# Two gain vectors moved from the activations: the input norm's g into the split of the transposed tiles, the heads' g into the split of the output weights

## The chip, the cores and the metric

The kernel runs on one core of a Trainium2 chip. The metric is the device time of one execution in microseconds (us), the median of several runs. Everything is float32; matrix products are made from a high and a low part of each operand, three TensorE passes per product (high × high, high × low, low × high), so each operand has to be split into two tiles, `h` and `l`.

## The reference

One layer of a streaming encoder, applied to 1024 prompt tokens and to 32 sample tokens with a state. Cut to what matters here:

```python
def rms_norm(x, g):
    y = x * rsqrt(mean(x * x, -1) + EPS)
    return y * g                              # g: one factor per feature (1024)

xn   = rms_norm(x, g_mix_pre)
proj = xn @ w_in                              # (tokens, 1024) @ (1024, about 3700)
...                                           # three groups of heads: GLA, HGRN2, mLSTM
o_a  = head_rms_norm(o_a, g_a) * silu(gr)     # per head: normed, times g_head, times a gate
o_b  = head_rms_norm(o_b, g_b) * silu(hg)
o_c  = head_rms_norm(h,   g_c) * sigmoid(mo)
x    = x + rms_norm(concat(o_a, o_b, o_c) @ w_out, g_mix_post)
x    = x + rms_norm(conv_ffn(rms_norm(x, g_ffn_pre)), g_ffn_post)
```

`g_mix_pre` scales the features over which the first product sums, and `g_head` the features over which the product with `w_out` sums. Each can therefore be applied to either operand of its product.

## The kernel before, in words

Tokens are handled in units of 128 (unit 8 holds the 32 sample tokens), and units in three groups: units 0 to 2, units 3 to 5, units 6, 7 and 8.

For each group the in-projection runs in stages. `scale_x` loads x of a unit (tokens on the partitions, 1024 features along), sums its squares on ScalarE (ACT), forms 1/rms on GpSimd (POOL: `rstd_of`, L221 and L222) and scales x on VectorE (DVE) by that column and by `gx`, a copy of g_mix_pre on every partition (L310 for unit 0, in two halves; L319 for the others). `norm_group` transposes the unit on TensorE, 128 features at a time and four such tiles to a PSUM bank, and splits each bank into `xh` (ACT, L333) and `xl` (DVE, L334), 512 columns in one instruction each. Then come the products: `vg` makes eight blocks of 256 columns with tokens on the partitions (`vg_across` for the third group), `feat` makes tiles of 128 features. Blocks 4 to 7 are the gates. `vg_store` turns a gate's PSUM tile into `vth` (or `gth` in the third group) with tanh on ACT (L113, called at L437) and one or two DVE instructions (L440, L442), multiplies it on POOL by `gh`, half of g_head copied to every partition (L444, out to the tile `vg`), and stores it to `g_d` in DRAM with POOL's queue (L445). `vth` has one buffer, `gth` three, `vg` three. Values (blocks 0 to 3) are copied to `vg` by ACT and stored to `v_d`.

`scale_x` of the next group runs behind block 5 of a group: its Square and scaling are ordered behind the last tanh and the last DVE instruction of `vg_store` (`vgi`). The mixers of a group run interleaved with the in-projection of the next one; they read `g_d` back as `gt` and multiply the normed heads by it (L1019).

`gx` is loaded by ACT's DMA queue first of all (512 KB written), `gh` by SP's queue behind the constants (L652, 512 KB) and halved on DVE (L653). `out_weights` splits the eight tiles of w_out, 128 rows of 1024 each, into `woh` (ACT, L107 or L1075) and `wol` (DVE, L110 or L1077), one tile for each k of the first unit's product in the out-projection (`outproj`). `split` is the helper of L107 and L110; `mm3` that of L101 to L103.

The order of the instructions on each engine is worked out by a planner from a simulated timeline; `high_priority` and `issue_after` in the code bend it.

Of the kernel before, what the change touches and what calls it, by code (L numbers as in the profile page):

```python
# [8 lines left out]
F32 = mybir.dt.float32  # L9
# [3 lines left out]
AF = mybir.ActivationFunctionType  # L13
ALU = mybir.AluOpType
# [40 lines left out]
for _h in (0, 2, 1, 3, 4):  # L55
# [24 lines left out]

TC = dict(schedule_with_timeline_sim=True)
IN_NAMES = ["xp", "xs", "w_feat", "w_tok0", "w_tok", "w_out", "w_up", "w_dn", "vecs", "gcols", "grows", "wg",
            "mconv", "mcache", "fconv", "fcache", "s_gh", "s_c", "s_m", "rowb", "masks", "cf"]
# [8 lines left out]
def body(ctx: ExitStack, tc: tile.TileContext, a: dict):  # L92
# [12 lines left out]
    def split(hi, lo, src, eng=None, heng=None):  # L105
        if heng is None:
            act.copy(hi, src)  # L107
        else:
            heng.tensor_copy(hi, src)
        (eng or pool).tensor_tensor(lo, src, hi.bitcast(F32), op=ALU.subtract)  # L110
# [50 lines left out]
            sp.dma_start(t, src)  # L161
        return t

    gx = p1.tile([128, 1024], F32, name="gx")
    act.dma_start(gx, a["grows"][3:4, :].broadcast_to([128, 1024]))
# [86 lines left out]
    gh = p1.tile([128, 1024], F32, name="gh")  # L252

    cols_of, dcs_of, behind = {}, {}, {}
    HSET = (2, 0, 4, 5)
# [37 lines left out]
    def scale_x(g):  # L293
        for (u, off, n) in units_of(g):
            x = x_in.pop(u, None)
            x = load_x(u) if x is None else x
            if g == 0:
                jk = mx.tile([128, 1024], BF16, tag=("gt", "cat", "k")[u], name=f"jk{u}", bufs=1)
            else:
                jk = mx.tile([128, 1024], BF16, tag="qe", name=f"jk{u}", bufs=1)  # L300
            rs = p1.tile([128, 1], F32, tag="rs", name=f"rs{u}", bufs=2)
            if u == 0:
                ss = p1.tile([128, 2], F32, name="ss0")
                hs = slice(0, 512), slice(512, 1024)
                for i, c in enumerate(hs):
                    act.activation(jk[:, c], x[:, c], AF.Square, scale=1.0 / 32, accum_out=ss[:, i:i + 1])
                pool.tensor_scalar(rs, ss[:, 0:1], ss[:, 1:2], EPS, op0=ALU.add, op1=ALU.add)
                pool.tensor_tensor(rs, rs, mhalf[:, :1], op=ALU.pow)
                for c in hs:
                    dve.scalar_tensor_tensor(x[:, c], x[:, c], rs, gx[:, c], op0=ALU.mult, op1=ALU.mult)  # L310
                xn_of[u] = x
                yield
                continue
            ss = p1.tile([128, 1], F32, tag="ss", name=f"ss{u}", bufs=2)
            with tc.issue_after(vgi[0].ins) if vgi else ExitStack():
                act.activation(jk[:n], x[:n], AF.Square, accum_out=ss[:n])
            rstd_of(rs[:n], ss[:n], n, 1, 1024)
            with tc.issue_after(vgi[1].ins) if vgi else ExitStack():
                dve.scalar_tensor_tensor(x[:n], x[:n], rs[:n], gx[:n], op0=ALU.mult, op1=ALU.mult)  # L319
            xn_of[u] = x  # L320
            yield

    def norm_group(g, xh, xl):
        for (u, off, n) in units_of(g):
            x = xn_of[u]
            for hf in range(2):
                ps = psb.tile([128, 4, 128], F32, tag="big", name=f"xt{u}{hf}")
                for k in range(4):
                    c = 512 * hf + 128 * k
                    pe.transpose(ps[:, k, :n], x[:n, c:c + 128], ident[:n, :n])  # L330
                s = slice(4 * hf, 4 * hf + 4), slice(off, off + n)
                with tc.high_priority(offset=AHEAD):
                    act.copy(xh[(slice(None), *s)], ps[:, :, :n])  # L333
                    dve.tensor_tensor(xl[(slice(None), *s)], ps[:, :, :n], xh[(slice(None), *s)].bitcast(F32), op=ALU.subtract)  # L334
# [34 lines left out]
    def inproj(g, xh, xl, normed, scaled=None):  # L369
# [55 lines left out]
            return ws  # L425

        def vg_store(blk, u, off, n, ps):
            o = mx.tile([128, 256], F32, tag="vg", name=f"vg{u}_{blk}", bufs=3)
            t = t0 + off
            if blk < 4:  # L430
                vcopies.append(act.copy(o[:n], ps[:n, :256]))
                (act if g or blk else pool).dma_start(v_d[t:t + n, 256 * blk:256 * blk + 256], o[:n])
                return
            c0 = 256 * (blk - 4)
            th = gate[0].tile([128, 256], F32, tag="gth", name=f"gth{u}_{blk}", bufs=3) if gate else \
                mx.tile([128, 256], F32, tag="vth", name=f"vth{u}_{blk}", bufs=1)
            ia = tanh(th[:n], ps[:n, :256], 0.5)  # L437
            ns = min(max(704 - c0, 0), 256)
            if ns:
                iv = dve.scalar_tensor_tensor(th[:n, :ns], th[:n, :ns], 1.0, ps[:n, :ns], op0=ALU.add, op1=ALU.mult)  # L440
# [3 lines left out]
            pool.tensor_tensor(o[:n], th[:n], gh[:n, c0:c0 + 256], op=ALU.mult)  # L444
# [202 lines left out]
        dve.scalar_tensor_tensor(er[R], fm[R], -1.0, fm[R], op0=ALU.mult, op1=ALU.min)  # L647
        act.activation(er[R], er[R], AF.Exp)
        yield

        if g == 0:
            sp.dma_start(gh, a["grows"][2:3, :].broadcast_to([128, 1024]))  # L652
            dve.tensor_scalar(gh, gh, 0.5, None, op0=ALU.mult)  # L653


        for t, f in ((6, 1), (7, 2)):
            ps = feat(t)
# [409 lines left out]

    def out_weights(W):
        for k in range(8):
            if k < 2:  # L1070
                split(W[1][k], W[2][k], wo_raw[k], dve)
            else:

                with tc.issue_after(halves[0].ins):
                    act.copy(W[1][k], wo_raw[k])  # L1075
                with tc.issue_after(halves[1].ins):
                    dve.tensor_tensor(W[2][k], wo_raw[k], W[1][k].bitcast(F32), op=ALU.subtract)  # L1077
            yield


# [787 lines left out]
def _layout(i):  # L1868
# [28 lines left out]
    grows = np.stack([np.asarray(i["g_mix_post"])[0], np.asarray(i["g_ffn_post"])[0], np.asarray(i["g_head"])[0],  # L1897
                      np.asarray(i["g_mix_pre"])[0]])
    wg = np.zeros((128, 192), f)
    wg[64:80] = np.asarray(i["gla_w_gate"])[0]  # L1900

# [45 lines left out]
    r = dict(xp=np.asarray(i["x_prompt"])[0], xs=np.asarray(i["x_sample"])[0], w_feat=w_feat, w_tok0=w_tok0, w_tok=w_tok, w_out=w_out,  # L1947
             w_up=w_up, w_dn=w_dn, vecs=vecs, gcols=gcols, grows=grows, wg=wg, mconv=mconv, mcache=mcache, fconv=fconv,
             fcache=fcache, s_gh=s_gh, s_c=s_c, s_m=s_m, rowb=rowb, masks=masks, cf=cf)
    return {k: np.ascontiguousarray(v) for k, v in r.items()}  # L1950
# [43 lines left out]
```

## Time and profile before

| | |
|---|---|
| median of 3 runs | 1357.33 us (1355.49 to 1357.98) |
| profiled execution, first to last instruction | 1355.3 us |
| TensorE busy | 1310.8 us, 97% |
| VectorE (DVE) busy | 1025.2 us, 76% |
| ScalarE (ACT) busy | 709.8 us, 52% |
| GpSimd (POOL) busy | 317.6 us, 23% |
| mean granted TensorE clock | 0.983 of full speed |
| DMA | 269.72 MB, mean 199 GB/s |

The profiled execution's own time is known as its span only; the median of the timed runs lies 2.0 us above that. In rows of the timeline the columns are start, duration, engine, line, operation, output and inputs, how many were merged, and in brackets how long the engine had been idle before and what released it. In rows of a line's instructions the three durations are the shortest, the median and the longest in ns, then the first and the last start in us and the shapes. PE is TensorE's matmuls, PEld its weight loads.

### The profile page before, as it was taken

How to read it: one execution, taken by the hardware profiler on the slowest of the kernel's cores; microseconds unless marked ns; L12 is line 12 of the kernel's file. 1: busy time of each engine (PE TensorE's matmuls, PEld its weight loads, DVE VectorE, ACT ScalarE, POOL GpSimd, SP SyncE). 2: the span in 40 equal slices, each digit the busy share in tenths (PEclk: the TensorE clock that was granted, in tenths of full speed). 3: DMA queues.
4: the chain of work that ended last, by engine and by line, in shares of the span. 5: the costliest groups of instructions: out<-in, count | busy, mean ns of one | idle time of the engine just before them, and what ended most of it. 6: DMA issues, size and time to landing. Idle time of an engine off the chain costs nothing.

```text
span 1355.3 us, 29229 instructions
## 1 busy us (share of the span) xinstructions
PE 1310.8 (97%) x11472; PEld 1196.7 (88%) x11472; DVE 1025.2 (76%) x1921; ACT 709.8 (52%) x1362; POOL 317.6 (23%) x530
## 2 busy tenths in 40 slices
PE   6999999999999999999999999999999999999997
PEld 5999889998888887767899999999999996678885
DVE  5795649768598678876998888888888876499566
ACT  5555556555574555435654554545554545454552
POOL 4532303135032254213211212111111110010005
PEclk9999999999998989989999999999999999999998
DMA  9799778886879963454315457536455239645435
GB/s 342 241 358 363 265 244 258 278 281 211 292 230 308 336 201 125 142 182 103 128 48 188 134 133 189 134 111 180 120 147 154 82 127 397 254 161 146 141 102 124
DMA packets 126881, 269.72 MB, mean 199 GB/s; under 512 B 24167, under 2 KB 59143, under 8 KB 126663
## 3 DMA queue, kind: packets, MB, share of 16 engines
q1 hardware_dynamic: 113111, 244.78, 53.2%
q0 software_dynamic: 9120, 18.62, 7.3%
q10 hardware_dynamic: 4512, 4.46, 1.0%
q8 instruction: 90, 1.47, 0.5%
q14 instruction: 48, 0.39, 0.1%
HBM read 206.72 MB, written 86.18 MB: 216 GB/s over the span
## 4 chain that ended last, share of the span: by engine, by line
PE 63%; DVE 5%; DMA 3%; ACT 3%; issue 2%; POOL 1%; SPq 0%; DVEq 0%; POOLq 0%; ACTq 0%
PE pux L103 5%; PE pux L102 5%; PE pux L101 5%; PE puw L101 3%; PE puw L103 3%; PE puw L102 3%; PE q L101 3%; PE q L102 3%; PE q L103 3%; PE x L101 2%; PE x L102 2%; PE x L103 2%; PE puz L103 2%; PE puz L101 2%; PE puz L102 2%
## 5 line engine op out<-in xcount | busy, mean ns | idle before, releaser
L1409 DVE SCALAR_TENSOR_TENSOR y<-uu,fconv_sb,y 128x1060 f32<-128x1060 f32 x88 | 116.2, 1320 | 36.8 <-ACT y L1407 36.2
L1345 ACT COPY c<-pux 128x272 f32<-128x272 f32 (+1 forms) x132 | 49.3, 375 | 50.5 <-PE pux L103 49.8
L1407 ACT ACTIVATE y<-uu,fconv_sb 128x1060 f32<-128x1060 f32 x44 | 56.1, 1275 | 8.5 <-POOL uu L1403 7.8
L101 PE MATMUL pv<-wt_0h,xh 128*128 128x256 f32 (+1 forms) x192 | 56.3, 293 | 3.6 <-DVE xl L334 1.6
L103 PE MATMUL zp<-woh,cl 128*128 128x512 f32 (+1 forms) x144 | 57.7, 401 | 1.5 <-DVE cl L1106 1.5
L1406 POOL COPY fhalo<-uu 128x2 f32<-128x2 f32 x44 | 16.6, 376 | 180.7 <-DVE uu L1350 180.6
L101 PE MATMUL zp<-woh,ch 128*128 128x512 f32 (+1 forms) x144 | 57.8, 410 | 0.8 <-ACT ch L1105 0.8
L102 PE MATMUL zp<-wol,ch 128*128 128x512 f32 (+1 forms) x144 | 57.9, 402 | 0.0
L103 PE MATMUL pv<-wt_1h,xl 128*128 128x256 f32 (+1 forms) x192 | 55.1, 287 | 0.0
L103 PE MATMUL pv<-wt_0h,xl 128*128 128x256 f32 (+1 forms) x192 | 55.0, 286 | 0.0
L102 PE MATMUL pv<-wt_0l,xh 128*128 128x256 f32 (+1 forms) x192 | 54.8, 286 | 0.0
L101 PE MATMUL pv<-wt_1h,xh 128*128 128x256 f32 (+1 forms) x192 | 54.7, 285 | 0.0
L102 PE MATMUL pv<-wt_1l,xh 128*128 128x256 f32 (+1 forms) x192 | 54.4, 283 | 0.0
L1585 POOL TENSOR_TENSOR gss<-gss 128x1 f32<-128x1 f32 (+1 forms) x9 | 8.2, 906 | 185.0 <-ACT gjk L1578 185.0
L221 POOL TENSOR_SCALAR hrs<-hss 128x5 f32<-128x5 f32 (+3 forms) x27 | 10.1, 375 | 176.5 <-DVE hss L1015 172.6
L831 DVE COPY_PREDICATED P<-masks_sb,sc 128x352 f32<-128x352 int32 (+3 forms) x53 | 37.9, 715 | 5.9 <-PE sc L744 5.0
L101 PEld LDWEIGHTS pv<-wt_0h,xh 128*128 128x128 f32 x192 | 36.4, 190 | 5.3 <-DVE xl L334 2.1
L1403 POOL COPY uu<-uu 128x2 f32<-128x2 f32 x44 | 28.0, 637 | 38.8 <-DVE uu L1350 37.8
L101 PEld LDWEIGHTS pv<-wt_1h,xh 128*128 128x128 f32 x192 | 36.2, 189 | 0.7 <-issue 0.6
L222 POOL TENSOR_TENSOR hrs<-hrs,mhalf 128x5 f32<-128x5 f32 (+3 forms) x27 | 36.2, 1341 | 2.2
L103 PEld LDWEIGHTS pv<-wt_0h,xl 128*128 128x128 f32 x192 | 36.5, 190 | 0.2
L102 PEld LDWEIGHTS pv<-wt_0l,xh 128*128 128x128 f32 x192 | 36.5, 190 | 0.1
(1743 smaller groups left out, 5321.0 us busy)
## 6 DMA issues: line engine op xcount, KB each, us to landing
wrP<-in_w_dn SPq DMA_DIRECT2D x27, 512.0 KB, 4.4
h_d<-y SPq DMA_DIRECT2D x22, 530.0 KB, 3.7
ht<-h_d SPq DMA_DIRECT2D x22, 530.0 KB, 10.5
wt_0r<-in_w_tok SPq DMA_DIRECT2D x21, 512.0 KB, 5.7
wt_1r<-in_w_tok SPq DMA_DIRECT2D x21, 512.0 KB, 6.3
ws_d<-in_w_dn POOLq DMA_DIRECT2D x20, 512.0 KB, 8.9
wrP<-ws_d SPq DMA_DIRECT2D x20, 512.0 KB, 4.0
wt_0l<-lt_d SPq DMA_DIRECT2D x14, 512.0 KB, 4.5
```

The costliest lines, as they stand in the source:

```text
L101: pe.matmul(ps, lh[0], rh[0], start=first, stop=False, **kw)
L102: pe.matmul(ps, lh[0], rh[1], start=False, stop=False, **kw)
L103: return pe.matmul(ps, lh[1], rh[0], start=False, stop=last, **kw)
L221: pool.tensor_scalar(out, ss, 1.0 / width, eps, op0=ALU.mult, op1=ALU.add)
L222: pool.tensor_tensor(out, out, mhalf[:n, :cols], op=ALU.pow)
L831: dve.copy_predicated(dst, mk.broadcast_to([n, 11, *mk.shape[2:]]), src)
L1345: kept[name] = act.copy(t, ps)
L1403: pool.tensor_copy(u[:, GAP_P:GAP_P + 2], u[:, GAP_S - 2:GAP_S])
L1406: behind["POOL"] = pool.tensor_copy(fhalo[:, j, :], u[:, NCOL - 2:NCOL])
L1407: act.activation(y, u, AF.Identity, scale=fconv[:, j, 2:3], bias=fconv[:, j, 3:4])
L1409: dve.scalar_tensor_tensor(y, uu[i][:, s:s + NCOL], fconv[:, j, s:s + 1], y, op0=ALU.mult, op1=ALU.add)
L1585: pool.tensor_tensor(ss[:n, 0:1], ss[:n, 2:3], ss[:n, 3:4], op=ALU.add)
```

## The change

Both gains become columns: `gin` is [128, 2, 8], one column for each tile of 128 features, for g_mix_pre (`gmix`) and g_head (`ghead`, halved once on DVE). x is scaled by 1/rms alone. After the transposes features lie on the partitions, so g_mix_pre is applied as a per-partition factor while the tile is split; the split of a bank becomes four pairs of instructions of 128 columns. g_head is applied in the split of w_out's rows. The gates are stored as DVE leaves them, from one tile (`vg` with four buffers, or `gth` with three), which values use too.

```diff
-    gx = p1.tile([128, 1024], F32, name="gx")
-    act.dma_start(gx, a["grows"][3:4, :].broadcast_to([128, 1024]))
+    gin = cp.tile([128, 2, 8], F32, name="gin_sb")
+    act.dma_start(gin, a["gin"])
+    gmix, ghead = gin[:, 0], gin[:, 1]
...
+    dve.tensor_scalar(ghead, ghead, 0.5, None, op0=ALU.mult)
...
                 for c in hs:
-                    dve.scalar_tensor_tensor(x[:, c], x[:, c], rs, gx[:, c], op0=ALU.mult, op1=ALU.mult)
+                    dve.tensor_scalar(x[:, c], x[:, c], rs, None, op0=ALU.mult)
...
-                dve.scalar_tensor_tensor(x[:n], x[:n], rs[:n], gx[:n], op0=ALU.mult, op1=ALU.mult)
+                dve.tensor_scalar(x[:n], x[:n], rs[:n], None, op0=ALU.mult)
...
-                s = slice(4 * hf, 4 * hf + 4), slice(off, off + n)
                 with tc.high_priority(offset=AHEAD):
-                    act.copy(xh[(slice(None), *s)], ps[:, :, :n])
-                    dve.tensor_tensor(xl[(slice(None), *s)], ps[:, :, :n], xh[(slice(None), *s)].bitcast(F32), op=ALU.subtract)
+                    for k in range(4):
+                        c, gk = (slice(None), 4 * hf + k, slice(off, off + n)), gmix[:, 4 * hf + k:4 * hf + k + 1]
+                        act.activation(xh[c], ps[:, k, :n], AF.Copy, scale=gk)
+                        dve.scalar_tensor_tensor(xl[c], ps[:, k, :n], gk, xh[c].bitcast(F32), op0=ALU.mult, op1=ALU.subtract)
...
-            o = mx.tile([128, 256], F32, tag="vg", name=f"vg{u}_{blk}", bufs=3)
+            o = gate[0].tile([128, 256], F32, tag="gth", name=f"gth{u}_{blk}", bufs=3) if gate else \
+                mx.tile([128, 256], F32, tag="vg", name=f"vg{u}_{blk}", bufs=4)
...
-            th = gate[0].tile([128, 256], F32, tag="gth", name=f"gth{u}_{blk}", bufs=3) if gate else \
-                mx.tile([128, 256], F32, tag="vth", name=f"vth{u}_{blk}", bufs=1)
+            th = o
...
-            pool.tensor_tensor(o[:n], th[:n], gh[:n, c0:c0 + 256], op=ALU.mult)
-            pool.dma_start(g_d[t:t + n, c0:c0 + 256], o[:n])
+            pool.dma_start(g_d[t:t + n, c0:c0 + 256], th[:n])
...
-        if g == 0:
-            sp.dma_start(gh, a["grows"][2:3, :].broadcast_to([128, 1024]))
-            dve.tensor_scalar(gh, gh, 0.5, None, op0=ALU.mult)
...
         for k in range(8):
-            if k < 2:
-                split(W[1][k], W[2][k], wo_raw[k], dve)
-            else:
-                with tc.issue_after(halves[0].ins):
-                    act.copy(W[1][k], wo_raw[k])
-                with tc.issue_after(halves[1].ins):
-                    dve.tensor_tensor(W[2][k], wo_raw[k], W[1][k].bitcast(F32), op=ALU.subtract)
+            gk = ghead[:, k:k + 1]
+            with tc.issue_after(halves[0].ins) if k > 1 else ExitStack():
+                act.activation(W[1][k], wo_raw[k], AF.Copy, scale=gk)
+            with tc.issue_after(halves[1].ins) if k > 1 else ExitStack():
+                dve.scalar_tensor_tensor(W[2][k], wo_raw[k], gk, W[1][k].bitcast(F32), op0=ALU.mult, op1=ALU.subtract)
             yield
```

More of the change, by code (lines that the diff above doesn't have):

```diff
@@ L249, in small @@
         return t if len(shape) == 1 else t.rearrange("p (a b) -> p a b", b=shape[1])
-    gh = p1.tile([128, 1024], F32, name="gh")
     cols_of, dcs_of, behind = {}, {}, {}
@@ L1896, in _layout @@
     gcols = np.asarray(i["g_ffn_pre"])[0].reshape(8, 128).T
-    grows = np.stack([np.asarray(i["g_mix_post"])[0], np.asarray(i["g_ffn_post"])[0], np.asarray(i["g_head"])[0],
-                      np.asarray(i["g_mix_pre"])[0]])
+    grows = np.stack([np.asarray(i["g_mix_post"])[0], np.asarray(i["g_ffn_post"])[0]])
+    gin = np.stack([np.asarray(i[k])[0].reshape(8, 128).T for k in ("g_mix_pre", "g_head")], 1)
     wg = np.zeros((128, 192), f)
@@ L1946, in _layout @@
             cf[r0:r0 + dk, 876 + 2 * (t // 3) + (r0 // 32 % 2 if dk == 32 else 0)] = 1.0
-    r = dict(xp=np.asarray(i["x_prompt"])[0], xs=np.asarray(i["x_sample"])[0], w_feat=w_feat, w_tok0=w_tok0, w_tok=w_tok, w_out=w_out,
+    r = dict(xp=np.asarray(i["x_prompt"])[0], xs=np.asarray(i["x_sample"])[0], w_feat=w_feat, w_tok0=w_tok0, w_tok=w_tok, gin=gin, w_out=w_out,
              w_up=w_up, w_dn=w_dn, vecs=vecs, gcols=gcols, grows=grows, wg=wg, mconv=mconv, mcache=mcache, fconv=fconv,
```

2 lines of the change are left out of this document (1 added, 1 removed).

## The prediction

> **What bounds the kernel now.** I read the page's busy table first, then the busy time by stretch, then TensorE's waits inside the stretches that the edits touch, and last the single instructions.
>
> ```profile
> span 1355.3 us, 29229 instructions
> PE 1310.8 (97%) x11472; PEld 1196.7 (88%) x11472; DVE 1025.2 (76%) x1921; ACT 709.8 (52%) x1362; POOL 317.6 (23%) x530
> ...
> 0.00:22.00 22.00, 11.69 (x72) 10.31 (x72) 13.82 (x32) 11.75 (x23) 8.83 (x24) 1.00 0.90 303
> 22.00:100.00 78.00, 77.59 (x490) 74.66 (x491) 60.35 (x78) 43.91 (x72) 36.58 (x26) 1.00 0.90 316
> 100.00:150.00 50.00, 48.47 (x463) 47.83 (x463) 32.46 (x61) 27.43 (x57) 16.84 (x25) 0.97 0.91 322
> 150.00:300.00 150.00, 148.93 (x1689) 139.36 (x1688) 103.19 (x236) 83.26 (x161) 32.69 (x47) 0.99 0.81 270
> 300.00:350.00 50.00, 46.71 (x673) 42.06 (x672) 38.46 (x96) 27.67 (x66) 24.07 (x31) 1.00 0.65 210
> 350.00:500.00 150.00, 144.07 (x1949) 132.38 (x1948) 114.97 (x309) 88.27 (x204) 44.97 (x68) 0.97 0.83 277
> ```
>
> After the stretch and its length come the busy times of PE, PEld, DVE, ACT and POOL, the granted clock, the DMA share and GB/s. TensorE is busy 97% of the span and none of its matmuls goes away, so only its idle time can be won: 1355.3 − 1310.8 = 44.5 us. The edits lie before 515 us. There TensorE idles 10.3 us in the first 22 us, 0.4 up to 100, 1.5 in 100 to 150, 3.3 in 300 to 350 and 5.9 in 350 to 500. The first and the two boundaries between token groups (around 142 and 327 us) are where the edited lines run. The median of the runs, 1357.33, is 2.0 us above the profiled span; I carry that over unchanged.
>
> **The start.** TensorE can do nothing until the first rows are normed and transposed.
>
> ```profile
> 0.72 0.41 ACTq L165 DMA_DIRECT2D gx<-in_grows  x1
> 7.05 0.63 ACT L306 ACTIVATE jk<-x 128x512 bf16<-128x512 f32 x1 [0.19 <-DMA x<-in_xp]
> 8.87 1.41 DVE L310 SCALAR_TENSOR_TENSOR x<-x,rs,gx 128x512 f32<-128x512 f32 x2 [4.59 <-POOL rs L308]
> 9.68 1.97 PE L330 MATMUL xt<-ident,x 128*128 128x128 f32 x8 [9.68 <-DVE x L310]
> 17.46 0.40 PE L101 MATMUL pv<-wt_0h,xh 128*128 128x282 f32 x1 [0.25 <-DVE xl L334]
> 20.25 1.05 ACT L107 CAST wf_8h<-wf_8r 128x1024 fp32r<-128x1024 f32 x1 [2.02 <-DMA wf_8r<-in_w_feat]
> 22.18 0.40 PE L101 MATMUL pv<-wt_0h,xh 128*128 128x282 f32 x1 [0.44 <-ACT vg L431]
> ```
>
> The DMA queues between 2 and 4 us (packets, MB, share of the engines):
>
> ```profile
> q10 hardware_dynamic: 72, 0.29, 47.6%
> q1 hardware_dynamic: 83, 0.17, 43.9%
> ```
>
> q10 carries gx, q1 carries x: the broadcast of a row of g takes as much of the DMA engines as the data that TensorE waits for. The diff replaces it (512 KB) by gin (8 KB) and drops gh's 512 KB too.
>
> Removed from the path: (a) With q10's half, q1 would deliver the 512 KB of x up to 1.7 us earlier (0.17 MB in 2 us became double). The second half's Square cannot go before the first's is over, so I take 1.1 us of it; the bounds are 0 and 1.7. (b) The scaling loses its second tensor: these rows price it.
>
> ```profile
> L310 DVE SCALAR_TENSOR_TENSOR x<-x,rs,gx x2: 746/748/751, 8.9 to 9.5; 128x512 f32<-128x512 f32 x2
> L319 DVE SCALAR_TENSOR_TENSOR x<-x,rs,gx x8: 1272/1284/1755, 12.1 to 309.1; 128x1024 f32<-128x1024 f32 x7, 32x1024 f32<-32x1024 f32 x1
> L653 DVE TENSOR_SCALAR gh<-gh x1: 689/689/689, 17.9 to 17.9; 128x1024 f32<-128x1024 f32 x1
> L333 ACT CAST xh<-xt x18: 265/586/609, 10.8 to 343.2; 128x512 fp32r<-128x512 f32 x16, 128x128 fp32r<-128x128 f32 x2
> L334 DVE TENSOR_TENSOR xl<-xt,xh x18: 284/688/714, 11.4 to 344.7; 128x512 fp32r<-128x512 f32 x16, 128x128 fp32r<-128x128 f32 x2
> L838 ACT ACTIVATE qe<-q,cf_sb x36: 304/388/404, 135.7 to 546.3; 128x128 f32<-128x128 f32 x32, 128x32 f32<-128x32 f32 x4
> 154.18 1.28 ACT L838 ACTIVATE qe<-q,cf_sb 128x128 f32<-128x128 f32 x4 [0.19 <-DVE Qz L865]
> ```
>
> A scaling by a column (L653) takes 0.69 us where L319 takes 1.28: 0.6 us less per unit of 128 tokens, about 0.3 less for each half of the first unit. L653 itself goes: 0.69.
>
> Added: each half of a unit (L333, L334) becomes four ACT instructions of 128x128 with a column as scale and four DVE ones. L838 is the same form on ACT: 0.39 each, 1.28 for four, where one cast is 0.59. That is 0.7 us more ACT per half, 12.6 us in 18 halves. On DVE the 128x128 form of L334 is 0.28, plus 0.06 for the column (748 of L310 against 688 of L334, both 512 wide): 0.34. Neighbours overlap by 0.09 (the two of L310 take 1.41, not 1.50), so four take 4 × 0.34 − 3 × 0.09 = 1.1 us against 0.69: 0.4 more per half. DVE's total is nearly even: 9 × 0.6 + 0.7 = 6.1 removed, 18 × 0.4 = 7.2 added.
>
> Against that, matmuls go by feature tile: TensorE can take tile 0 after 0.39 + 0.34 us instead of 0.59 + 0.69, and three passes over a tile keep it busy for some 0.47 us (77.59 us / 490 matmuls between 22 and 100, times 3), which ACT's 0.32 sustains.
>
> DVE is busy almost without a gap from 8.87 to the wait at 17.46. The start comes 1.1 + 0.3 earlier; two later scalings give 1.2, three halves take 1.2, and the first piece is there some 0.5 sooner: 1.9. At 22.18 TensorE waits for ACT, which sat 2.02 us on the transfer of wf_8r; that stands in the queue behind 1 MB that is gone, 3.3 us at the 316 GB/s of 22 to 100. ACT's additional 5 × 0.7 = 3.5 us are paid there. I take **−2.0 us** for the start; bounds −3.3 (all of the transfer time) and +0.5 (ACT's extra decides). From 22 to 100 TensorE has no idle time, so what is won stays, unless weights come late: their DMA runs at a share of 0.90, but it is 1 MB ahead as well.
>
> **The group boundaries.** vg_store's product with gh on POOL goes; its tile vth had one buffer, the new one has four.
>
> ```profile
> 137.22 1.28 DVE L319 SCALAR_TENSOR_TENSOR x<-x,rs,gx 128x1024 f32<-128x1024 f32 x1 [0.47 <-POOL rs L222]
> 140.09 1.28 DVE L319 SCALAR_TENSOR_TENSOR x<-x,rs,gx 128x1024 f32<-128x1024 f32 x1 [0.44 <-POOL rs L222]
> 137.27 1.28 POOL L221 TENSOR_SCALAR rs<-ss 128x1 f32<-128x1 f32 x1
> 138.63 0.87 POOL L444 TENSOR_TENSOR vg<-vth,gh 128x256 f32<-128x256 f32 x1
> 142.63 0.58 PE L101 MATMUL pv<-wt_0h,xh 128*128 128x256 f32 x1 [1.53 <-DVE vth L440]
> 325.99 0.80 PE L744 MATMUL oi<-C,mqz 128*64 128x65 f32 x20 [0.96 <-DVE cat L1017]
> 328.54 0.38 ACT L113 ACTIVATE vth<-pv 128x256 f32<-128x256 f32 x1 [1.08 <-POOL vg L444]
> 328.98 0.66 PE L330 MATMUL xt<-ident,x 128*128 128x128 f32 x4 [0.73 <-ACT vth L113]
> 332.75 0.40 PE L101 MATMUL pv<-wt_0h,xh 128*128 128x282 f32 x1 [1.39 <-DVE xl L334]
> L444 POOL TENSOR_TENSOR vg<-vth,gh x24: 717/732/1656, 118.8 to 334.1; 128x256 f32<-128x256 f32 x24
> L444 POOL TENSOR_TENSOR vg<-gth,gh x12: 714/736/985, 472.8 to 497.0; 128x256 f32<-128x256 f32 x8, 32x256 f32<-32x256 f32 x4
> DMA to landing us min/median/max: 1.8/4.6/6.7
> ```
>
> At 142.63 TensorE waits for a PSUM bank that DVE's L440 must empty; L440 stands on DVE behind the scaling of 140.09, which waits for POOL's rs; and POOL had L444 (0.87) and an L221 that lasted 1.28 us for one column, exactly as long as the scaling beside it. Without L444 and with scalings of 0.7, rs is there 0.87 + 0.6 sooner and the scaling is 0.6 shorter: 2.0 us, more than the wait of 1.53. I take **−1.5**, bounds −1.5 and 0.
>
> A rule bears on that L221. The Trainium skill, "SBUF — State Buffer", "SBUF: two separate sides", says that an exclusive lock on a shared port pair blocks GpSimd while VectorE runs an instruction with two SBUF inputs or one in a 2-port mode, and counts tensor_scalar among the ops that can enter such a mode. The row agrees for two inputs; by the rule L221 would still be held for 0.7 us, which is what I count, and without the lock rs would come up to 0.7 us earlier still, to no effect on a wait that is gone already.
>
> At 328.98 the transposes wait for tanh of vth, tanh for the product on POOL (the one buffer): 0.73 goes. At 332.75 (1.39, first xh and xl of the group) the first piece comes about 0.5 sooner. The 0.96 at 325.99 hangs on the mixers and stays. **−1.2**; bounds −3.1 (all three go) and +0.7 (a half's extra ACT time in the path).
>
> In the third group the tile (gth, three buffers) is now held until its transfer has landed, 4.6 us after issue. Its three tiles are issued in a burst each 6 to 8 us, so the next tanh finds them free or waits up to 1.4 us on ACT, with ACT's casts of w_out queued behind it: 0, bounds 0 and +1.4. POOL's 36 × 0.73 = 26 us are off the path otherwise.
>
> **The weights of the out-projection.**
>
> ```profile
> L1075 ACT CAST woh<-wor x6: 1039/1040/1052, 497.5 to 508.1; 128x1024 fp32r<-128x1024 f32 x6
> L1077 DVE TENSOR_TENSOR wol<-wor,woh x6: 1207/1220/1226, 501.9 to 509.2; 128x1024 fp32r<-128x1024 f32 x6
> ```
>
> The column makes eight casts 0.09 longer each and eight subtractions 0.06 (1.28 against 1.22): 0.5 us on DVE, which is dense there. I take **+0.2**, bounds 0 and +1.2. The remaining 12 halves add 0.7 on ACT and 0.4 on DVE where ACT is 55% busy (83.26 of 150 us): **+0.3**, bounds 0 and +2. Halving ghead is one small op early: 0.
>
> Sum: −2.0 − 1.5 − 1.2 + 0.2 + 0.3 = −4.2. Span 1351.1, median **1353.1**.
>
> **Rivals.** (1) The waits at the boundaries stay: behind L440 and the tanh stands DVE's own queue of mixer work, and TensorE's next wait takes over. Only the start is won: 1353.1 + 2.7 = 1355.8, no change within 0.2% (2.7 us, about what runs that spread over 2.5 us can tell). For it: DVE has 38.46 of 50 us in 300 to 350. Against: both waits name the edited chain.
> (2) More goes: start −3.3, boundaries −1.5 and −2.1, +0.5 of costs: −6.4, so 1350.9 to 1349.
> (3) Slower: ACT becomes the bound of the split, because the matmuls get going only after the last of four pieces. Then each half on the path costs 0.7. With the start at −2.0 and nothing won later, 12 later halves cost 8.4: +6.4, so 1363; it turns slower than before by more than 2.7 us from 7 halves on (−2.0 + 4.9), at 1360. For it: TensorE waits for xl four times in the trace. Against: ACT idles 45% there and mixer matmuls fill TensorE. The Trainium skill, "VectorE: DVE Perf Modes", section on the TRN2 errata, speaks for this rival: a fixed cost per instruction on VectorE and ScalarE, hence its advice of tiles of 512 elements or more, where the diff goes from 512 to 128.
>
> **Chances.** Forecast 0.47 (own range 1351 to 1354.6), rival 1 0.25, rival 2 0.13, rival 3 0.15. Faster by over 0.2% (below 1354.6): 0.60; within: 0.25; slower: 0.15. The range 1349 to 1358.5 takes in rivals 1 and 2 and the lower edge of uncertain costs; it leaves out most of rival 3.
>
> **What would show it.** First transposes near 8.3 us, the third unit's first matmul near 20; no ACT wait on POOL at tanh and no 1.5 us wait for L440 near 140; L444 gone; ACT's busy time up about 13 us and POOL's down about 26; TensorE's busy time unchanged. Wrong would make it: xh's first reader waiting for the fourth piece, tanh waiting for g_d, or a different order of the mixers' work that opens gaps where there were none, since the program's order is planned from costs and each of these edits changes them.

## The result, and the profile after

The changed kernel is slower: 1373.16 us (median of 4 runs, 1364.94 to 1381.72) against 1356.94 us for the kernel before, timed beside it (4 runs); ratio 1.013, 95% interval 1.0085 to 1.0175. Forecast were 1353.1 us and a range of 1349 to 1358.5. The runs spread by more than the kernel before does, and the longer ones have the lower granted clock (a span of 1363.1 us at 0.988, of 1380.0 at 0.976); the profiled execution, 1371.6 us at 0.981, lies between. The lower clock is only a part of the loss: at 0.988 the changed kernel took 1364.94 us where six runs of the kernel before, timed beside the experiments, took 1351.1 to 1354.8, and at 0.983 it took 1372.95 against 1359.15. At equal clock that is some 12 to 14 us.

The page's busy table and the busy time by stretch of the changed kernel, columns as before (stretch, length, PE, PEld, DVE, ACT, POOL, clock, DMA share, GB/s):

```profile
span 1371.6 us, 29325 instructions
PE 1322.2 (96%) x11472; PEld 1200.8 (88%) x11472; DVE 1023.7 (75%) x1975; ACT 724.0 (53%) x1416; POOL 284.4 (21%) x494
...
0.00:22.00 22.00, 10.36 (x47) 8.77 (x48) 13.19 (x39) 13.03 (x30) 10.10 (x24) 1.00 0.89 309
100.00:150.00 50.00, 50.00 (x424) 50.00 (x423) 29.99 (x56) 27.70 (x55) 11.34 (x19) 1.00 1.00 363
300.00:350.00 50.00, 47.91 (x691) 43.50 (x690) 37.96 (x110) 29.61 (x72) 16.64 (x25) 0.90 0.62 209
350.00:500.00 150.00, 141.20 (x1849) 128.01 (x1848) 109.11 (x291) 84.72 (x198) 31.66 (x48) 0.98 0.79 270
```

Much of the forecast's list is there. The wait of 1.5 us near 142 us is gone (100 to 150 is now full), POOL has 33 us less, ACT 14 us more, DVE is even. But the first stretch got through 47 matmuls where it was 72, and 350 to 500 has 2.9 us less TensorE work in it.

How far each kernel has come at 700 us shows the loss in one row. From there on TensorE is busy without a gap in both kernels (300.00 of 300 us up to 1000). The row of the kernel before first, then that of the changed kernel:

```profile
0.00:700.00 700.00, 667.32 (x7038) 604.46 (x7039) 522.93 (x1100) 387.74 (x788) 218.45 (x304) 0.97 0.71 238
```
```profile
0.00:700.00 700.00, 662.38 (x6898) 591.82 (x6898) 506.83 (x1132) 391.44 (x827) 183.00 (x262) 0.97 0.70 235
```

140 matmuls are missing at 700 us. Afterwards each kernel does about 820 in 100 us, so that is 17 us: the whole difference of the spans (16.3). Only 4.9 us of it is additional idle time before 700; the rest sits in TensorE's busy time, which is up by 11.4 us with the same 11472 matmuls. All of that rise is in the first products of the three groups, the 216 matmuls of 282 columns that read the split tiles: counting each up to the start of the next, they take 44.8 us where they took 32.4. Busy is not the same as getting on, as the start shows. TensorE, then VectorE, then ScalarE in the changed kernel's timeline:

```profile
8.20 1.97 PE L330 MATMUL xt<-ident,x 128*128 128x128 f32 x8 [8.20 <-DVE x L310]
10.71 0.60 PE L458 MATMUL pv<-wt_0h,xh 128*128 128x282 f32 x1 [0.54 <-ACT xh L334]
13.06 0.60 PE L458 MATMUL pv<-wt_0h,xh 128*128 128x282 f32 x1 [1.75 <-ACT xh L334]
13.85 0.60 PE L458 MATMUL pv<-wt_0h,xh 128*128 128x282 f32 x1 [0.19 <-ACT xh L334]
15.30 1.07 PE L458 MATMUL pv<-wt_1h,xh 128*128 128x282 f32 x3 [0.85 <-ACT xh L334]
21.36 0.30 PE L103 MATMUL pv<-wt_0h,xl 128*128 128x282 f32 x1
```
```profile
10.66 1.03 DVE L110 TENSOR_TENSOR wt_1l<-wt_1r,wt_1h 128x846 fp32r<-128x846 f32 x1
11.61 0.74 DVE L110 TENSOR_TENSOR wt_2l<-wt_2r,wt_2h 128x564 fp32r<-128x564 f32 x1
12.27 0.60 DVE L335 SCALAR_TENSOR_TENSOR xl<-xt,gin_sb,xh 128x128 fp32r<-128x128 f32 x2
```
```profile
10.29 0.62 ACT L334 ACTIVATE xh<-xt,gin_sb 128x128 fp32r<-128x128 f32 x2
12.64 0.63 ACT L334 ACTIVATE xh<-xt,gin_sb 128x128 fp32r<-128x128 f32 x2 [0.47 <-DVE xl L335]
```

The transposes start at 8.20, 1.5 us earlier than before, as forecast. ScalarE makes the first piece of each of the unit's two banks at 10.29. Then it is to make the second piece, but that starts at 12.64, released by VectorE's first `xl`, and VectorE came to that only at 12.27, behind two splits of weights. TensorE gets its tiles of `xh` at 10.71, 13.06, 13.85 and 15.30, one at a time.

Two things make such a stretch long without making it idle. A matmul that stands alone counts as busy for its whole record, 0.60 us here, while those in a row overlap: the records of 0.30 us around 21.36 follow each other every 0.13 us. And TensorE runs at half its pace in part of the time. At the start it does so in both kernels, up to some 13 us before and some 19 us now: there even matmuls in a row without any wait take 0.44 us, 0.24 apart, although the clock column says 1.00 for these 22 us. In the changed kernel the half pace comes back inside the splits of the second and third group, and there the clock column shows it. Two stretches and one matmul in a row of the changed kernel, then the same place in the third group of the kernel before:

```profile
169.00:172.00 3.00, 3.00 (x19) 2.91 (x14) 2.04 (x4) 0.00 (x0) 0.00 (x0) 0.54 0.03 5
340.00:348.50 8.50, 8.05 (x74) 6.67 (x74) 6.44 (x21) 5.54 (x17) 2.63 (x4) 0.50 0.33 116
345.55 0.44 PE L101 MATMUL pv<-wt_1h,xh 128*128 128x282 f32 x1
```
```profile
332.75:342.00 9.25, 9.25 (x116) 8.54 (x117) 8.43 (x27) 6.71 (x21) 3.36 (x4) 1.00 0.48 169
333.25 0.30 PE L101 MATMUL pv<-wt_0h,xh 128*128 128x282 f32 x1
```

Of the 216 records 57 are longer than 0.43 us, 5 in the kernel before; a late matmul at full pace takes 0.39 (at 355.68 below). Why the clock was low in just these stretches no run isolates. Up to 700 us its mean is 0.97 in both kernels (rows above), so the half pace says where the busy time lies, and is not by itself the net loss.

Why does ScalarE wait for VectorE at all, when `xh` needs nothing that VectorE makes? The four tiles of a half lie in one PSUM bank, and both engines read them. In the changed program, ScalarE's second piece of a bank carries a wait for VectorE's first, the third for the second, and so on. The Trainium skill, "PSUM — Partial Sum Buffer", in the section on PSUM bank collisions, says that two engines must not access the same bank and the same 32 partitions at once, reads against reads included, and that it takes semaphores by bank, not by address, to keep them apart. The trace agrees as far as it goes: where one half is alone, no piece of ScalarE's overlaps one of VectorE's (ScalarE, then VectorE, changed kernel); what an overlap would do, no run here shows.

```profile
19.31 0.37 ACT L334 ACTIVATE xh<-xt,gin_sb 128x128 fp32r<-128x128 f32 x1 [0.80 <-PE xt L330]
20.10 0.37 ACT L334 ACTIVATE xh<-xt,gin_sb 128x128 fp32r<-128x128 f32 x1 [0.42 <-DVE xl L335]
```
```profile
19.72 0.35 DVE L335 SCALAR_TENSOR_TENSOR xl<-xt,gin_sb,xh 128x128 fp32r<-128x128 f32 x1 [3.43 <-ACT xh L334]
20.51 0.35 DVE L335 SCALAR_TENSOR_TENSOR xl<-xt,gin_sb,xh 128x128 fp32r<-128x128 f32 x1 [0.44 <-ACT xh L334]
```

A pair takes 0.79 us, 0.37 and 0.35 and the way between, with one of the two engines always idle. Over the whole kernel (instructions of the two lines, and what ended the idle time before them: us, times):

```profile
L334 ACT ACTIVATE xh<-xt,gin_sb x72: 279/367/392, 10.3 to 365.0; 128x128 fp32r<-128x128 f32 x64, 128x32 fp32r<-128x32 f32 x8
  DVE xl L335: 13.9, 23
```
```profile
L335 DVE SCALAR_TENSOR_TENSOR xl<-xt,gin_sb,xh x72: 241/344/356, 12.3 to 365.4; 128x128 fp32r<-128x128 f32 x64, 128x32 fp32r<-128x32 f32 x8
  ACT xh L334: 15.6, 23
```

The third group, where the mixers load both engines, shows the other half of it. ScalarE, VectorE and TensorE between 350 and 356 us:

```profile
350.31 0.62 ACT L334 ACTIVATE xh<-xt,gin_sb 128x128 fp32r<-128x128 f32 x2 [0.49 <-PE xt L330]
352.37 0.63 ACT L334 ACTIVATE xh<-xt,gin_sb 128x128 fp32r<-128x128 f32 x2 [1.43 <-DVE xl L335]
355.40 0.63 ACT L334 ACTIVATE xh<-xt,gin_sb 128x128 fp32r<-128x128 f32 x2 [2.40 <-DVE xl L335]
```
```profile
352.00 0.59 DVE L335 SCALAR_TENSOR_TENSOR xl<-xt,gin_sb,xh 128x128 fp32r<-128x128 f32 x2
352.52 0.92 DVE L826 COPY_PREDICATED P<-masks_sb,sc 128x352 f32<-128x352 int32 x1
353.24 0.89 DVE L904 TENSOR_TENSOR kw<-mi,cols 64x256 f32<-64x256 f32 x2
354.14 0.46 DVE L904 TENSOR_TENSOR kw<-sm,cols 64x64 f32<-64x64 f32 x2
354.62 0.49 DVE L906 TENSOR_TENSOR w<-w,sm 128x320 f32<-128x320 f32 x1
355.02 0.60 DVE L335 SCALAR_TENSOR_TENSOR xl<-xt,gin_sb,xh 128x128 fp32r<-128x128 f32 x2
```
```profile
355.68 0.39 PE L103 MATMUL pv<-wt_0h,xl 128*128 128x282 f32 x1 [0.96 <-DVE xl L335]
```

VectorE has six other instructions in its queue between two pairs of pieces, so ScalarE's next pieces start 3.0 us after the ones before. The instructions of a unit's split get spread out. Three counts from the traces make that comparable between kernels: the time from a unit's first piece of `xh` to its last of `xl`, summed over the nine units; the number of other instructions that stand between those pieces on each engine; and the length of the stage, from the first transpose of a group to the start of its last, summed over the three groups.

| kernel | first to last piece, nine units, us | others between, ScalarE / VectorE | stage, three groups, us | median, us |
|---|---|---|---|---|
| before (whole banks) | 31.3 | 20 / 22 | 40.1 | 1356.9 |
| changed: high, low, high, low | 57.2 | 36 / 67 | 66.3 | 1373.2 |
| four high, four low (below) | 43.8 | 19 / 28 | 43.3 | 1353.7 |
| two and two (below) | 52.7 | 35 / 57 | 53.5 | 1362.0 |
| the cut alone, in alternation (below) | 51.5 | 36 / 52 | 63.9 | 1374.7 |

The stages of the three groups took 11.8, 13.0 and 15.3 us before; now they take 16.9, 22.1 and 27.3. On two engines the stage goes with the medians, but for the kernel before, which lacks the heads' gain; the first two counts do not fully, since two and two and the cut alone have nearly the same ones and medians 13 us apart.

### The profile page after: what moved, and what is told of

It reads as the page before. It is cut to its first block, busy times and chain, and to the rows that moved or that the text cites. A ratio compares the mean times of both kernels' runs of the same rounds, so it can differ in the third digit from the quotient of the medians.

```text
span 1371.6 us, 29325 instructions
## 1 busy us (share of the span) xinstructions
PE 1322.2 (96%) x11472; PEld 1200.8 (88%) x11472; DVE 1023.7 (75%) x1975; ACT 724.0 (53%) x1416; POOL 284.4 (21%) x494
## 4 chain that ended last, share of the span: by engine, by line
PE 78%; DVE 11%; ACT 5%; DMA 3%; issue 2%; POOL 1%; SPq 0%; DVEq 0%; POOLq 0%; ACTq 0%
PE pux L102 5%; PE pux L103 5%; PE pux L101 5%; PE pv L101 4%; PE pv L103 4%; PE pv L102 4%; PE puw L102 3%; PE puw L101 3%; PE puw L103 3%; PE q L101 3%; PE q L102 3%; PE q L103 3%; PE x L101 2%; PE sc L739 2%; PE x L102 2%; PE x L103 2%
## 5 line engine op out<-in xcount | busy, mean ns | idle before, releaser
L103 PEld LDWEIGHTS pv<-wt_1h,xl 128*128 128x128 f32 x192 | 37.0, 193 | 0.8 <-issue 0.2
L102 PEld LDWEIGHTS pv<-wt_1l,xh 128*128 128x128 f32 x192 | 37.1, 193 | 0.1
```

The source lines that it names most:

```text
L102: pe.matmul(ps, lh[0], rh[1], start=False, stop=False, **kw)
L103: return pe.matmul(ps, lh[1], rh[0], start=False, stop=last, **kw)
```

## The experiments

In the expectations, theory A is the alternation on one bank, B the number and length of the pieces, C the heads' part or the planned order. All ratios are to the kernel before, timed beside each.

**The heads' part alone.** `gx` and the split of whole banks stay; the rest of the diff is done.

```diff
-                dve.tensor_scalar(x[:n], x[:n], rs[:n], None, op0=ALU.mult)
+                dve.scalar_tensor_tensor(x[:n], x[:n], rs[:n], gx[:n], op0=ALU.mult, op1=ALU.mult)
...
-                    for k in range(4):
...
+                    act.copy(xh[(slice(None), *s)], ps[:, :, :n])
+                    dve.tensor_tensor(xl[(slice(None), *s)], ps[:, :, :n], xh[(slice(None), *s)].bitcast(F32), op=ALU.subtract)
```

> Only the heads' g is moved (into the split of the output weights, gates stored unmultiplied from a tile with four buffers); the input norm is as before, with gx. Theory A (the loss is the alternation of ScalarE and VectorE on the pieces of one PSUM bank, 4 x 0.79 us instead of 1.27 us a half): no loss here, 1352 to 1357 us, since 36 products of 0.73 us leave GpSimd and the 1.5 us wait near 142 us goes. Theory B (the pieces cost by their number, 0.7 us more ScalarE time a half): the same as A. Theory C (the loss is from the heads' part or from the other order of the mixers that follows from it): 1365 us or more.

Measured: 1349.55 us, ratio 0.9962 (0.9942 to 0.9982). This is the best kernel of the study, faster than both. C falls. The rows of the boundary in this kernel, the stretch before it and TensorE's first product of the third group:

```profile
100.00:150.00 50.00, 50.00 (x430) 49.63 (x431) 29.23 (x53) 28.48 (x55) 10.86 (x18) 1.00 0.98 354
```
```profile
328.34 0.40 PE L101 MATMUL pv<-wt_0h,xh 128*128 128x282 f32 x1 [1.05 <-ACT xh L335]
```

The wait near 142 us is gone, and the third group's first product comes at 328.3 instead of 332.8.

**The input part alone.** The converse: columns for g_mix_pre, the heads' part as before.

```diff
-            pool.dma_start(g_d[t:t + n, c0:c0 + 256], th[:n])
+            pool.tensor_tensor(o[:n], th[:n], gh[:n, c0:c0 + 256], op=ALU.mult)
+            pool.dma_start(g_d[t:t + n, c0:c0 + 256], o[:n])
```

> Only the input norm's g is moved (column, pieces of 128); the heads are as before, with gh on GpSimd. A and B: nearly the whole loss, 1368 to 1376 us. C: 1357 us or less.

Measured: 1380.7 us, ratio 1.0184 (1.0155 to 1.0214); the changed kernel's loss without its gain.

**Four high parts, then four low parts.** The changed kernel with the same 72 pairs, the same shapes and factors; only the order in a bank is another, so that ScalarE does not wait for VectorE within it.

```diff
-                    for k in range(4):
...
-                        act.activation(xh[c], ps[:, k, :n], AF.Copy, scale=gk)
-                        dve.scalar_tensor_tensor(xl[c], ps[:, k, :n], gk, xh[c].bitcast(F32), op0=ALU.mult, op1=ALU.subtract)
...
+                    for k, (c, gk) in enumerate(cs4):
+                        act.activation(xh[c], ps[:, k, :n], AF.Copy, scale=gk)
+                    for k, (c, gk) in enumerate(cs4):
+                        dve.scalar_tensor_tensor(xl[c], ps[:, k, :n], gk, xh[c].bitcast(F32), op0=ALU.mult, op1=ALU.subtract)
```

> The changed kernel with the same 72 pairs of instructions, but all four ScalarE pieces of a half before its four VectorE pieces, so there is one hand-over in place of four. A: a half takes 1.3 + 1.1 = 2.4 us instead of 3.2, no ScalarE wait for a piece of xl, and half or more of the 16 us comes back: 1358 to 1365 us. B: no change against the changed kernel, 1370 us or more, since number and length of the instructions are the same. C: no change either.

Measured: 1353.65 us, ratio 0.9989 (0.9973 to 1.0004). All of the loss is gone, more than was expected. B falls as the cause: the number and length of the pieces are what they were. Its pieces at the start, ScalarE and VectorE, and the row at 700 us:

```profile
10.43 2.17 ACT L334 ACTIVATE xh<-xt,gin_sb 128x128 fp32r<-128x128 f32 x8
```
```profile
12.47 1.12 DVE L336 SCALAR_TENSOR_TENSOR xl<-xt,gin_sb,xh 128x128 fp32r<-128x128 f32 x4
13.58 1.12 DVE L336 SCALAR_TENSOR_TENSOR xl<-xt,gin_sb,xh 128x128 fp32r<-128x128 f32 x4
```
```profile
0.00:700.00 700.00, 666.53 (x7081) 602.27 (x7082) 527.73 (x1164) 400.04 (x847) 191.06 (x270) 0.99 0.71 237
```

ScalarE does a unit's eight pieces in one go, and VectorE takes each bank in one go. At 700 us there are 183 matmuls more than in the changed kernel.

**Two and two.** Between these: high, high, low, low, twice per bank.

```diff
-                    for k in range(4):
+                    for k0 in (0, 2):
...
+                        for k, c, gk in cs2:
+                            act.activation(xh[c], ps[:, k, :n], AF.Copy, scale=gk)
+                        for k, c, gk in cs2:
+                            dve.scalar_tensor_tensor(xl[c], ps[:, k, :n], gk, xh[c].bitcast(F32), op0=ALU.mult, op1=ALU.subtract)
```

> The changed kernel with the pieces of a half in the order two on ScalarE, two on VectorE, two, two: one ScalarE wait for VectorE inside a half, where the changed kernel has three and the run with four and four has none. A (each hand-over costs): in proportion, a third of the way from 1354 to 1373, 1357 to 1364 us. B (number and length of the pieces): as 1354 us, since all three kernels have the same 72 pairs; that the run with four and four gave 1354 already speaks against B.

Measured: 1361.99 us, ratio 1.0052 (1.0038 to 1.0066). With none, one and three waits of ScalarE for VectorE in a bank the medians are 1353.65, 1361.99 and 1373.16. A part of the middle one is clock: its four runs were granted 0.982 to 0.985, the kernel before 0.987 in the mean.

**The cut alone.** The kernel before, with nothing of the change but the cut of each bank into four alternating pairs; no factor, `gx` and `gh` as they were.

```diff
-                    act.copy(xh[(slice(None), *s)], ps[:, :, :n])
-                    dve.tensor_tensor(xl[(slice(None), *s)], ps[:, :, :n], xh[(slice(None), *s)].bitcast(F32), op=ALU.subtract)
+                    for k in range(4):
+                        c = (slice(None), 4 * hf + k, slice(off, off + n))
+                        act.copy(xh[c], ps[:, k, :n])
+                        dve.tensor_tensor(xl[c], ps[:, k, :n], xh[c].bitcast(F32), op=ALU.subtract)
```

> The kernel before with one edit: the split of a bank cut into four pairs of casts and subtractions of 128 columns, in alternation. No column as a factor, gx and gh as before. A: the whole loss and no gain, 1375 to 1382 us, like the input part alone (1380.7). If the loss needs the factor column or the other transfers at the start: 1360 us or less.

Measured: 1374.74 us, ratio 1.0147 (1.0132 to 1.0161). The cut in this order makes the loss by itself, at the clock of the kernel before (0.986 against 0.987 in the mean), and even though its pieces are shorter (row of ScalarE's line in this kernel):

```profile
L334 ACT CAST xh<-xt x72: 185/265/299, 10.7 to 365.1; 128x128 fp32r<-128x128 f32 x64, 128x32 fp32r<-128x32 f32 x8
```

**Whole banks without g_mix_pre.** The changed kernel with whole banks split in one pair: the change without the price of the cut. It leaves out the multiplication by g_mix_pre.

```diff
-                        act.activation(xh[c], ps[:, k, :n], AF.Copy, scale=gk)
-                        dve.scalar_tensor_tensor(xl[c], ps[:, k, :n], gk, xh[c].bitcast(F32), op0=ALU.mult, op1=ALU.subtract)
+                    act.copy(xh[(slice(None), *s)], ps[:, :, :n])
+                    dve.tensor_tensor(xl[(slice(None), *s)], ps[:, :, :n], xh[(slice(None), *s)].bitcast(F32), op=ALU.subtract)
```

> The changed kernel with the split of a whole bank in one instruction on each engine, as before; the multiplication by g_mix_pre is left out altogether. It prices what the rest of the change gives without the pieces. A and B: the terms forecast for the start and the boundaries without the costs, 1350 to 1355 us. C: 1365 us or more.

Measured: 1358.83 us, ratio 1.003 (1.0016 to 1.0045), above what was expected. Up to 470 us it is ahead of the kernel before by some 2 us; it falls behind in the out-projection, where TensorE's largest wait is one that the kernel with the heads' part alone does not have at this size (0.9 us there):

```profile
560.00:580.00 20.00, 13.25 (x101) 10.38 (x98) 17.53 (x45) 9.34 (x22) 7.54 (x8) 0.74 0.36 110
PE oi L738 <- DVE cat L1011: 4.9, 1, 4.9
```

That is a place which the edit does not touch. It looks like another planned order of the mixers' work; no run isolates it, so it stays open.

**g spread over the partitions by TensorE.** The best kernel, with the 512 KB broadcast of `gx` replaced by 4 KB and a product with a column of ones.

```diff
+    act.dma_start(gx[0:1], a["grows"][2:3, :])
...
+        pe.matmul(gp, ones, gx[0:1, 512 * hf:512 * hf + 512], start=True, stop=True)
+        act.copy(gx[:, 512 * hf:512 * hf + 512], gp)
```

> The heads' part alone, and gx no longer as a broadcast transfer of 512 KB: one row of 4 KB is loaded and copied to all partitions by a TensorE product with ones and two ScalarE copies. If the transfer of gx is what delays the first transposes by 1.5 us and the rest of the start follows: first transposes near 8.6 us and 1348 us, 1 to 2 us below the heads' part alone (1349.6). If other work takes over after the start: as the heads' part alone.

Measured: 1356.86 us, ratio 1.0016 (1.0001 to 1.0031). The first transposes come at 7.2 us, 2.6 earlier than in the best kernel, but the first product with `wf_8h` comes at 25.7 against 25.6: what is won at the first transpose is lost within the first 25 us. The same wait of 4.9 us in the out-projection is there as well.

**Two banks in turn.** To tell a lock on one bank from the hand-over as such: both halves are transposed first, and the pieces are taken from the two banks in turn.

```diff
+                for j in range(8):
+                    k, hf = j // 2, j % 2
...
+                    act.activation(xh[c], ps2[hf][:, k, :n], AF.Copy, scale=gk)
+                    if last:
+                        dve.scalar_tensor_tensor(*last, op0=ALU.mult, op1=ALU.subtract)
+                    last = xl[c], ps2[hf][:, k, :n], gk, xh[c].bitcast(F32)
```

> The changed kernel with as many hand-overs between ScalarE and VectorE as it has, but over two PSUM banks: both halves of a unit are transposed first, and the pieces are taken in turn from one half's bank and the other's, so that while VectorE reads a piece of one bank ScalarE reads one of the other. Each of ScalarE's pieces still waits for VectorE's previous piece of its own bank. Theory A (what costs is that the two engines cannot work on one bank at once, so that a pair of pieces takes the sum of both, 0.79 us): a unit's eight pairs take about 8 x 0.4 = 3.2 to 3.6 us instead of 6.3, so most of the 20 us between the changed kernel and the one with four and four come back: 1353 to 1361. Rival (what costs is the hand-over as such, a piece that queues behind other work of its engine each time, whichever bank it is): 1366 to 1376, as the changed kernel.

Measured: 1371.0 us, ratio 1.0139 (1.0102 to 1.0176). It tells nothing apart: as far as the split goes, the planned order on both engines has the same counts as that of the changed kernel (36 and 67 others between), which already took a unit's two banks in turn, as its rows from 10.29 on show. It is in effect a second timing of the changed kernel.

**All pieces on VectorE.** No hand-over inside a bank; still high, low, high, low.

```diff
-                        act.activation(xh[c], ps[:, k, :n], AF.Copy, scale=gk)
+                        dve.tensor_scalar(xh[c], ps[:, k, :n], gk, None, op0=ALU.mult)
```

> The changed kernel with both instructions of each of the 72 pairs on VectorE, still high part, low part, high part, low part of one bank; ScalarE has no part in the split, so nothing is handed over inside a bank. The two-bank run showed nothing, since the changed kernel already took a unit's two banks in turn: the same instructions in the same order. This one separates what is left. Theory A1 (the serial sum of a bank is what costs: a pair one after the other, 0.79 us in the changed kernel): a pair still takes about 0.3 + 0.34 less an overlap, some 0.6 us, so a half some 2.3 to 2.5 us on one engine, and most of the loss stays: 1364 to 1374. Theory A2 (what costs is each hand-over, a piece that has to wait behind other work of two engines in turn): no hand-over is left, and the time is near that of four and four, 1353 to 1362, the upper part of it because VectorE gets 72 x 0.3 = 21 us more to do and ScalarE 26 us less.

Measured: 1377.59 us, ratio 1.0162 (1.0112 to 1.0211): slower than either expectation. A2 falls: the loss does not need a hand-over between engines. VectorE in the third group:

```profile
343.60 0.34 DVE L335 SCALAR_TENSOR_TENSOR xl<-xt,gin_sb,xh 128x128 fp32r<-128x128 f32 x1
343.86 0.34 DVE L334 TENSOR_SCALAR xh<-xt,gin_sb 128x128 fp32r<-128x128 f32 x1
344.12 0.68 DVE L860 TENSOR_TENSOR Qz<-x,qe 128x128 f32<-128x128 f32 x3
344.72 0.16 DVE L1037 SCALAR_TENSOR_TENSOR den<-hn 128x5 f32<-128x5 f32 x1
344.80 0.42 DVE L851 TENSOR_TENSOR Ld<-x,k 128x256 f32<-128x256 f32 x1
345.13 0.34 DVE L335 SCALAR_TENSOR_TENSOR xl<-xt,gin_sb,xh 128x128 fp32r<-128x128 f32 x1
```

Other work stands between the pieces here too, and the nine units take 64.4 us from first to last piece.

**All on VectorE, four and four.** The same instructions on the same engine, in the order that helped.

```diff
-                    for k in range(4):
...
-                        act.activation(xh[c], ps[:, k, :n], AF.Copy, scale=gk)
...
+                    for k, (c, gk) in enumerate(cs4):
+                        dve.tensor_scalar(xh[c], ps[:, k, :n], gk, None, op0=ALU.mult)
+                    for k, (c, gk) in enumerate(cs4):
                         dve.scalar_tensor_tensor(xl[c], ps[:, k, :n], gk, xh[c].bitcast(F32), op0=ALU.mult, op1=ALU.subtract)
```

> The same 144 instructions on VectorE as in the run with all pieces on VectorE, of the same length and on the same engine; only their order in a bank is changed: four high parts, then four low parts, instead of high, low, high, low. Theory A1 (the serial sum of a bank on one engine is what costs): the sum is the same, so is the time: 1372 to 1382. Theory A3 (what costs is a chain of short instructions of which each waits for the one before, on one engine or on two, because the planned order puts other work into the gaps and the engine takes it in order; in the run before this one other work stood between nearly all pieces of the third group): four and four have no such chain, the pieces stand together, and most of the loss goes: 1353 to 1364. Between 1364 and 1372 both have a share.

Measured: 1372.76 us, ratio 1.0126 (1.0103 to 1.0149). The nine units now take 52.1 us instead of 64.4, but the time falls by only 4.8 us between the medians, and the intervals of the two ratios overlap. A3 falls as the only cause: order without two engines does not bring the time back. (The order itself holds in seven of the nine units; in the other two the planner put high pieces of the second bank among the low ones of the first.) A1's range holds the time, at its lower edge, but the serial sum of a bank is not enough either: on two engines, four and four take 1.14 + 1.12 us, mostly one after the other, as long as on one engine, and none of the loss is there. VectorE is also busy for 1040 us in both of these runs against 1024 in the changed kernel, and what this load costs was not measured by itself.

What the runs settle: on two engines the loss is the split of a bank by pieces in alternating order, and it goes when ScalarE has all of a bank's pieces behind it before VectorE begins, so that each engine goes through a bank in one go. It does not go because the two engines then work at once more often: ScalarE's and VectorE's pieces run at the same time for 4.1 us in all in the good order, and for 7.4 in the changed kernel. What the runs leave open: how much of the loss is the wait itself (0.79 us a pair where a half is alone) and how much the other work that gets between the pieces (six instructions and 2.5 us in the rows at 352.52), since the two come together in every alternating run on two engines; what share TensorE's half pace has; and why VectorE alone stays some 16 us slower even in the good order.

## Why the prediction was wrong

**The step that failed** is the one on what matmuls get from pieces: "TensorE can take tile 0 after 0.39 + 0.34 us instead of 0.59 + 0.69, [...] which ACT's 0.32 sustains". It took ScalarE to run at its own pace, four pieces in 1.28 us, with VectorE one piece behind. In the program that came of it, each of ScalarE's pieces of a bank but the first waits for VectorE's piece before it. The price of 0.7 us on ACT and 0.4 on DVE per half, and with it the +0.3 for the other twelve halves, rests on that pace. In its place a half alone takes 4 × 0.79 = 3.2 us where one cast and one subtraction took 0.59 + 0.69 = 1.3, and where other work steps in, ScalarE's next pieces come 3.0 us after the ones before. The group stages grow by 5.1, 9.1 and 12.0 us, 26 in all, of which 16 to 17 reach the end.

**The durations themselves were right.** Four pieces on ScalarE were forecast at 1.28 us, four on VectorE at 1.1; in four-and-four order a bank takes 1.14 and 1.12. So the terms were measured well, and the error is not in any of them, but in the assumption that each engine goes through its four pieces without a wait for the other.

**The forecast number describes the other order.** With four and four the kernel takes 1353.65 us, near the forecast of 1353.1. That the sum is met there is luck, since its terms are not. The heads' part was to bring −1.5 − 1.2 + 0.2 = −2.5; alone it brings 5.7 us between the medians (ratio 0.9962, so 2.4 to 7.9 us). The casts and subtractions of the out-projection's weights got longer by 0.09 and 0.06 us each, as forecast (1.13 and 1.28). The input part was to bring −2.0 at the start; the kernel with both parts in the good order isn't faster than that with the heads' part alone (1353.65 against 1349.55), so at best it brings nothing.

**"What is won stays" failed too.** The first transposes came at 8.20 us (forecast 8.3), but the third unit's first matmul at 25.56 (forecast near 20, before 22.18). In the good order it comes at 21.12, yet from 22 to 100 us TensorE then has gaps which it didn't have before (73.81 of 78 us against 77.59), 2.5 us of them in two waits for VectorE's `q` (L574): the work behind the split sets the pace there. The run in which g is spread by TensorE shows the same more sharply, with 2.6 us won and nothing left 18 us later.

**Right as forecast:** the wait near 142 us gone, no wait of tanh for POOL (at 326.94 tanh waits for TensorE's product), L444 gone, ACT 14 us up (forecast 13), POOL 33 us down (forecast 26). Wrong: TensorE's busy time unchanged; it rose by 11.4 us, in the first products of the groups.

**The rivals.** The third, slower, was the right side, at a chance of 0.15, with another mechanism: it had TensorE wait for the fourth piece, at 0.7 us a half. TensorE did get each piece as it came, and it was each piece that came late. By its price even eighteen halves would have cost 12.6 us, less than the loss. (Its own time, 1357.3 + 6.4, is 1363.7, where 1363 stands.) The page of the Trainium skill that was named for it, "VectorE: DVE Perf Modes", section on the TRN2 errata, advises against tiles below 512 elements for a fixed cost of each instruction that reads SBUF; ScalarE's pieces read PSUM. A cost of that kind is in the trace (four pieces take ScalarE 1.14 us, one cast of a whole bank 0.59). But the same 72 pairs of 128 in the good order take 1353.65 us where they take 1373.16 in alternation, so that cost is not what made the kernel slow; it may be a part of the 4.1 us by which the good order stays behind the heads' part alone.

## What to carry to other kernels

When an instruction that reads a whole PSUM bank is cut into pieces, look at who else reads that bank: two engines that took its pieces in turn were serialised here, and each turn was one more place where other work stepped in between. Let one engine finish the bank before the other begins. A sum of right durations says nothing about the time until it is asked which of them wait for each other. And ask of a busy engine how much work it got done: the number of matmuls started by 700 us showed the loss, TensorE's share of busy time (97% and 96%) did not.

## What was not expected of the hardware

Two reads of different columns of one bank, on two engines, cost 0.79 us per pair when ordered by semaphores, for 0.37 and 0.35 us of work: some 0.04 us from the end of one piece to the start of the next. TensorE's busy time is no measure of its work: the same 11472 matmuls were busy for 1303.4 us in the best kernel and for 1322.2 in the changed one. Matmuls of 282 columns came every 0.13 us in a row at full pace and every 0.24 at half pace, and one that stood alone was busy for 0.40 and 0.60. Half pace lasted for 8.5 us in the middle of a kernel with a mean clock of 0.981 (0.50 from 340 to 348.5), and at the start it shows in the durations alone, not in the clock column. And the first transposes can come 2.6 us earlier without the products of 18 us later coming earlier.
